# A hybrid encoder layer on one core: input weights loaded three units ahead, norms on VectorE, split tiles of the gated unit kept in DRAM, part of V made later, and w_down's squares spread out

## The chip, the cores and the metric

The kernel runs on one core of a Trainium2 chip. A core has a matrix engine (TensorE, PE in the profile; PEld is its weight load), VectorE (DVE), ScalarE (ACT), GpSimd (POOL), and SyncE (SP), which here only issues DMAs. Each engine works through a queue of its own in order; semaphores tie the queues together. Sixteen DMA engines move data between DRAM and the core's on-chip memory. The metric is the time of one execution on the device in microseconds.

## The reference

The layer computes, for a sequence of 2048 tokens of width 1024 and a memory of 256 tokens:

```python
y = rmsnorm(h, norm_mix_g) @ w_in            # 1024 -> 3*512 (q, k, v) + 2*512 (a, g)
q, k = partial_rotary(q), partial_rotary(k)  # 16 of 64 columns of each head
att = dilated_sliding_attention(q, k, v)     # patterns (128, 1), (512, 4), (2048, 16)
conv = silu(layernorm(conv31(a * sigmoid(g))))
h = h + concat(att, conv) @ w_out
h = h + softmax(xq @ xk.T / 16) @ xv @ w_xo  # xq of rmsnorm(h), xk and xv of rmsnorm(mem)
u = rmsnorm(h, norm_mlp_g) @ w_up            # 1024 -> 4096
h = h + square(relu(u)) @ w_down
out = rmsnorm(h, norm_final_g)
```

All inputs and outputs are float32. Attention has 8 heads of 64, its three patterns are merged with their log-denominators; cross attention has 4 heads of 256.

## The kernel before, in words

**Numbers as pairs.** A float32 product is made of three float16 products: each operand is scaled by a power of two and split into a hi and a lo part, and `mm3` (L392 to L394) issues hi·hi, hi·lo and lo·hi. So each weight tile of 128 output columns (a "raw" tile of 128 x 8 x 128, 0.5 MB) has to be loaded, scaled and split before TensorE can use it. For the input weights w_in the scale comes from the tile itself: `wscale` (L322) squares it and sums the squares on ScalarE (`wjunk`), a one-column matmul `p` (L198) sums over partitions, and a few small instructions of VectorE and GpSimd (`pow2`) make the scale. `wsplit16` (L345) then scales the tile in place on ScalarE (L349), casts it to the hi part (L351) and subtracts on GpSimd or VectorE (L352). For the later weights `wsplit2` (L379) does it in two instructions, with scales that come from sums of squares over whole matrices: `scan` reads w_up and w_out once for that (40 tiles, `sjunk`, L225) while the first stages run, and `scan_down` reads w_down (32 tiles, `sjunkd`, L247).

**Stages in time.** (1) Memory: the fold of w_xq, w_xk, w_xv and w_xo with the memory's norm into two matrices per head that are put into DRAM as ascr and bscr (results `pa`, `pb`, evicted into `eb`, squared for their scale at L670). (2) `xprep`: x is read in four blocks of 512 tokens; `rstd_nat` (L510) takes the squares of each row (`sumsq`, L505, `junk`), transposes of 128 x 128 (`xt`) turn it, VectorE multiplies it with gain and norm (`xv`, L540), ScalarE and GpSimd split it (`xh`, `xl`). `rb` and `rbs` are the norm broadcast over partitions. (3) The linear stage: `pipeline` (L700) runs units. A unit is one weight tile with what hangs on it: `glu` gives the units g and a of the four column groups c (their halves for token blocks 0, 1 here); `lin_qk` the units q and k, of which the pair named kr and qr holds the rotated columns of all heads, gathered from w_in in 64-byte pieces with eight DMAs each; `lin_v` (L775) the two halves of V, 256 columns each. Results go to DRAM (`uscr`, `kscr`, `qscr`, `qfar`, `vtok`). (4) The far stretch: attention of block 0 with its farthest pattern (`att(0)`; scores `s`, probabilities `sm`, transposes `pt`, its split `ph`, `pl`, output `opt`), in which the other halves of g and a (token blocks 2, 3), with their weights loaded, scaled and split again, serve as filler (`rest`). (5) Four times a `post` block of 512 tokens: w_out, cross attention (`x`, `xs`, `xp`), then w_up and w_down, with the attention and the convolution of the next block woven in. `scan_down` runs at the start of the first.

**What sets the order.** A step of a unit is what its generator does up to the next `yield`: load, square, scale, split, then matmuls. `pipeline` advances the next unit and the one after beside the current one, so that a load is two units ahead; the raw buffers are two. `weave(main, (side, rate))` advances a side generator by `rate` steps for each step of the main one. Within this, a scheduler of the framework puts the instructions of each engine in order by its own estimate of their times, except where `pinned` and `after` fix that a group is issued after the last marked instruction of an engine. All loads and nearly all stores go through SyncE's queue in that order; a store there waits at the head of the queue until its data is ready. Some stores of q and k are issued by ScalarE.

Of the kernel before, what the change touches and what calls it, by code (L numbers as in the profile page):

```python
# [10 lines left out]
F32 = mybir.dt.float32  # L11
# [10 lines left out]
P = 128  # L22
# [26 lines left out]
def hybrid_layer(ctx, tc, A, out):  # L49
# [68 lines left out]
    catl = [dr.tile([P, S], F16, name=f"catl{k}") for k in range(KC)]  # L118
    ascr = dr.tile([XH // 2, P, KC, 2 * NMEM], F32, name="ascr")
# [150 lines left out]
    def bounds():  # L270
# [9 lines left out]
        with ExitStack() as st:  # L280
# [9 lines left out]
            DVE.scalar_tensor_tensor(c[14], c[4], 4.0, c[14], op0=ALU.mult, op1=ALU.add)  # L290
# [32 lines left out]
    def wscale(raw, key):  # L323

        if key in tiles_scaled:
            yield
            return
        n = tiles_scaled[key] = 4 * len(tiles_scaled)
        q = lp.tile([P, 1024], BF16, tag="wjunk", name="wjunk")
        ACT.activation(q, raw.rearrange("p a b -> p (a b)"), AF.Square, accum_out=wsc[:, n + 3:n + 4])  # L330
# [14 lines left out]
    def wsplit16(raw, key, name, lo_eng=None, views=None):  # L345
        hi = wp.tile([P, 8, P], F16, tag="whi", name=f"whi_{name}", bufs=2)
        lo = wp.tile([P, 8, P], F16, tag="wlo", name=f"wlo_{name}", bufs=2)
        s = wcol(key, 0)
        ACT.activation(raw, raw, AF.Copy, scale=s)  # L349
        for of, to in views or ((lambda t: t,) * 2,):  # L350
            ACT.copy(to(hi), of(raw))  # L351
            (lo_eng or DVE).tensor_tensor(to(lo), of(raw), to(hi), op=ALU.subtract)  # L352
        return hi, lo
# [25 lines left out]
    def wsplit2(wp, raw, name, scale, bufs=2, shape=(P, 8, P)):  # L379
        hi = wp.tile(list(shape), F16, tag="whi", name=f"whi_{name}", bufs=bufs)  # L380
        lo = wp.tile(list(shape), F16, tag="wlo", name=f"wlo_{name}", bufs=bufs)
        ACT.activation(hi, raw, AF.Copy, scale=scale)  # L382
        DVE.scalar_tensor_tensor(lo, raw, scale, hi, op0=ALU.mult, op1=ALU.subtract)  # L383
        return hi, lo
# [94 lines left out]
    xna[2] = pool("x2", stack=mems, side="right")  # L479
    XH_ = {}  # L480
# [24 lines left out]
    def sumsq(sp, t, ss, j, n):  # L505

        for e in range(2):
            q = sp.tile([P, 512], BF16, tag="junk", name="junk", bufs=1)
            ACT.activation(q, t[e], AF.Square, accum_out=ss[:, n * e + j:n * e + j + 1])

    def rstd_nat(sp, nat, name):
        n = len(nat)
        ss = sp.tile([P, 8], F32, tag="ss", name=f"ss{name}", bufs=2)
        for j in range(n):
            sumsq(sp, nat[j], ss, j, n)
# [33 lines left out]
    def memory(sp):  # L549
# [24 lines left out]
        def wtiles(name, shape=(P, 8, P)):  # L574
            i = cnt[0] % 4
            cnt[0] += 1
            if i < 2:
                return [wp.tile(list(shape), dt, tag=t, name=f"m{t}_{name}", bufs=2)
# [121 lines left out]
    def pipeline(*units):  # L700

        for _ in range(4):
            next(units[0])
# [1143 lines left out]
```

## Time and profile before

| | us |
|---|---|
| median of 3 runs | 2853.81 (2852.42 to 2854.03) |
| the profiled execution | 2859.55 |
| its span | 2857.8 |
| TensorE busy | 2702.5 (95%) |
| VectorE busy | 2017.9 (71%) |
| ScalarE busy | 1379.2 (48%) |
| GpSimd busy | 489.6 (17%) |
| moved by DMA | 455.80 MB, mean 159 GB/s |

The times of the profile are those of one execution, counted from its first instruction. A "granted clock" below 1 means that TensorE ran below its full rate for part of the stretch. In a row of waits the engine that waits stands first, then what it waited for, then the total, the number and the longest. In a row of the timeline the bracket at the end is the idle time ahead of the instruction and what ended it.

### The profile page before, as it was taken

The numbers are of one execution on the slowest core, as the hardware profiler recorded it, in microseconds if no ns is written. First come the engines' busy times: TensorE is split into PE (matmuls) and PEld (weight loads), VectorE is DVE, ScalarE is ACT, GpSimd is POOL, SyncE is SP. The second block draws the span as 40 slices with busy tenths as digits, with TensorE's granted clock in tenths as the row PEclk, the third lists the DMA queues.
The fourth block names the chain that finished last, engine by engine and source line by source line (L and its number), as shares of the span: only waits on it lengthen the run. The fifth ranks groups of instructions, "written<-read, shape, count | busy, mean of one in ns | idle before, by whom it ended". The sixth has DMA issues, their size and how long they took to land.

```text
span 2857.8 us, 41763 instructions
## 1 busy us (share of the span) xinstructions
PE 2702.5 (95%) x15482; PEld 1486.6 (52%) x15482; DVE 2017.9 (71%) x3647; ACT 1379.2 (48%) x2295; POOL 489.6 (17%) x521
## 2 busy tenths in 40 slices
PE   8878799998887999999999999999999999999998
PEld 7744346666644555554554555455455544444443
DVE  6534664565567798756799886679979655579997
ACT  5776422265566444443454445345434444455443
POOL 1135442222210111130002202200201130000000
PEclk9989899999998999999999999999999999999999
DMA  9899985568896354454544454553445445323332
GB/s 273 245 266 282 252 206 150 137 171 215 218 274 213 103 142 132 137 147 119 169 128 127 132 147 125 158 165 110 136 135 142 126 147 158 105 82 103 118 118 67
DMA packets 629773, 455.80 MB, mean 159 GB/s; under 512 B 192733, under 2 KB 558225, under 8 KB 629056
## 3 DMA queue, kind: packets, MB, share of 16 engines
q1 hardware_dynamic: 588816, 429.19, 53.5%
q10 hardware_dynamic: 38528, 17.93, 2.5%
q0 software_dynamic: 2224, 6.01, 0.6%
q8 instruction: 122, 2.00, 0.3%
q14 instruction: 83, 0.68, 0.1%
HBM read 370.04 MB, written 82.98 MB: 159 GB/s over the span
## 4 chain that ended last, share of the span: by engine, by line
PE 48%; DVE 3%; issue 2%; DMA 2%; POOL 1%; ACT 0%; SPq 0%; POOLq 0%; DVEq 0%; ACTq 0%
PE dn L392 6%; PE dn L394 6%; PE dn L393 6%; PE up L392 6%; PE up L393 6%; PE up L394 6%; PE o L392 1%; PE o L394 1%; PE o L393 1%; PE xs L392 1%; PE xs L394 1%; PE xs L393 1%; PE s L1236 1%; PE pt L1014 1%; DVE cacc L409 1%
## 5 line engine op out<-in xcount | busy, mean ns | idle before, releaser
L392 PE MATMUL up<-mh,whi_u 128*128 128x512 f16 x1024 | 389.4, 381 | 7.5 <-ACT mh L1460 3.8
L409 DVE SCALAR_TENSOR_TENSOR cacc<-cu,cw,cacc 128x512 f32<-128x512 f32 x480 | 387.5, 807 | 5.6
L393 PE MATMUL up<-ml,whi_u 128*128 128x512 f16 x1024 | 389.1, 380 | 1.2 <-DVE ml L1461 1.2
L394 PE MATMUL up<-mh,wlo_u 128*128 128x512 f16 x1024 | 387.9, 380 | 0.0
L394 PE MATMUL dn<-hhh,wlo_d 128*128 128x512 f16 x768 | 291.3, 380 | 0.0
L393 PE MATMUL dn<-hhl,whi_d 128*128 128x512 f16 x768 | 290.8, 380 | 0.0
L392 PE MATMUL dn<-hhh,whi_d 128*128 128x512 f16 x768 | 283.8, 380 | 0.1
L382 ACT ACTIVATE whi_u<-raw_u,bd 128x1024 f16<-128x1024 f32 x128 | 146.8, 1147 | 257.3 <-PE dn L393 163.8
L382 ACT ACTIVATE whi_d<-raw_d,bd 128x1024 f16<-128x1024 f32 x100 | 114.9, 1149 | 263.3 <-PE up L393 229.3
L383 DVE SCALAR_TENSOR_TENSOR wlo_u<-raw_u,bd,whi_u 128x1024 f16<-128x1024 f32 x128 | 169.5, 1324 | 33.8 <-ACT whi_u L382 33.6
L1586 DVE SCALAR_TENSOR_TENSOR h<-dn,bd,h 128x512 f32<-128x512 f32 x192 | 140.4, 745 | 72.8 <-PE dn L394 72.7
L394 PEld LDWEIGHTS <-wlo_u 128*128 128x128 f16 x1024 | 100.4, 98 | 121.6 <-issue 2.7
L1007 DVE CUSTOM_DVE_ANT_0 sm<-s,mask 128x256 f32<-128x256 f32 (+1 forms) x384 | 127.1, 374 | 51.0 <-PE s L1236 31.6
L393 PEld LDWEIGHTS <-whi_u 128*128 128x128 f16 x1024 | 100.7, 98 | 119.0 <-issue 6.3
L392 PEld LDWEIGHTS <-whi_u 128*128 128x128 f16 x1024 | 100.8, 99 | 116.2 <-issue 2.7
L369 POOL TENSOR_TENSOR nr<-st_v,mhalf 128x4 f32<-128x4 f32 (+1 forms) x15 | 17.3, 1152 | 825.3 <-DVE st_v L365 825.3
L1570 DVE SCALAR_TENSOR_TENSOR rl<-up,ssumx 128x512 f32<-128x512 f32 x96 | 65.7, 689 | 124.7 <-PE up L394 124.6
L383 DVE SCALAR_TENSOR_TENSOR wlo_d<-raw_d,bd,whi_d 128x1024 f16<-128x1024 f32 x100 | 132.9, 1329 | 23.1 <-ACT whi_d L382 22.8
L1018 DVE TENSOR_TENSOR pl<-pt,ph 128x512 f16<-128x512 f32 x160 | 109.4, 685 | 55.4 <-ACT ph L1017 55.0
L1008 ACT ACTIVATE sm<-sm,o 128x256 f32<-128x256 f32 (+1 forms) x288 | 116.6, 453 | 52.2 <-DVE o L1007 51.6
L1017 ACT CAST ph<-pt 128x512 f16<-128x512 f32 x160 | 91.2, 573 | 82.4 <-PE pt L1014 82.4
L394 PEld LDWEIGHTS <-wlo_d 128*128 128x128 f16 x768 | 75.3, 98 | 89.4 <-issue 1.0
(541 smaller groups left out, 6776.6 us busy)
## 6 DMA issues: line engine op xcount, KB each, us to landing
raw_u<-in_w_up_dram SPq DMA_DIRECT2D x128, 512.0 KB
raw_d<-in_w_down_dram SPq DMA_DIRECT2D x100, 512.0 KB
scan<-in_w_up_dram SPq DMA_DIRECT2D x32, 512.0 KB
raw_o<-in_w_out_dram SPq DMA_DIRECT2D x32, 512.0 KB
scand<-in_w_down_dram SPq DMA_DIRECT2D x32, 512.0 KB
raw_a<-ascr SPq DMA_DIRECT2D x32, 512.0 KB
raw_b<-bscr SPq DMA_DIRECT2D x32, 512.0 KB
b<-in_w_down_dram SPq DMA_DIRECT2D x28, 512.0 KB
```

The costliest lines, as they stand in the source:

```text
L382: ACT.activation(hi, raw, AF.Copy, scale=scale)
L383: DVE.scalar_tensor_tensor(lo, raw, scale, hi, op0=ALU.mult, op1=ALU.subtract)
L392: PE.matmul(o, lh, rh, start=first, stop=False, skip_group_check=more)
L393: PE.matmul(o, lh, rl, start=False, stop=False, skip_group_check=more)
L394: last["pe"] = PE.matmul(o, ll, rh, start=False, stop=end, skip_group_check=more)
L409: DVE.scalar_tensor_tensor(acc, u[:, t:t + 512], cw[:, c, t:t + 1], acc, op0=ALU.mult, op1=ALU.add)
L1007: last["dve"] = DVE.tensor_tensor_reduce(dst, so, mask[:, 256 * m:256 * m + nk], 1.0, 3e38, ALU.add, ALU.min, mn)
L1008: last["act"] = ACT.activation(dst, dst, AF.Exp, bias=mn, scale=-1.0)
L1017: ACT.copy(ph, pt)
L1018: DVE.tensor_tensor(pl, pt, ph, op=ALU.subtract)
L1570: last["dve"] = DVE.scalar_tensor_tensor(r, pt, 0.0, rsb, op0=ALU.max, op1=ALU.mult)
L1586: last["dve"] = DVE.scalar_tensor_tensor(hs[m], pt, K_DN, hs[m], op0=ALU.mult, op1=ALU.add)
```

## The change

The change has eight parts.

1. Loads: three raw buffers in place of two; `pipeline` starts the load of unit i + 3 when unit i begins (units 0, 1 and 2 are advanced 4, 3 and 1 steps ahead of the first).
2. Squares and norms: `wscale` takes the largest square of each partition with one VectorE instruction in place of the sum on ScalarE; the same for the squares of `eb` (their bound's factor goes from 4 to 16 for it); the rows' sums of squares of token blocks 2 and 3 go to VectorE too.
3. Splits: q, k, g and a are split as the later weights are, by one scaled cast on ScalarE and one subtraction with scale on VectorE; only kr and qr keep the old form. Hi and lo part are the halves of one tile `ws` (two buffers). The memory stage's split tiles get a pool of their own.
4. The gated unit's eight split tiles of the first pass are stored into `gscr` in DRAM, and the second pass, in the far stretch, reads them (`wr_`) in place of loading, scaling and splitting.
5. V: of the second pair only token blocks 0 and 1 are made in the linear stage; its split weights are stored into `vscr`, read again (`wvr1`), and token blocks 2 and 3 are made as the first unit of the far stretch's filler.
6. Filler: the attention steps of the far stretch take 1.0 step of filler each in place of 0.75.
7. Rates of `scan` and of the first convolution steps in the linear stage.
8. `scan_down`: 1 step per step of the first 12 of the block, then 1.25 over the next 18, in place of 4 per step over 9 steps after those 12.

```diff
     def wscale(raw, key):
-        if key in tiles_scaled:
-            yield
-            return
         n = tiles_scaled[key] = 4 * len(tiles_scaled)
         q = lp.tile([P, 1024], BF16, tag="wjunk", name="wjunk")
-        ACT.activation(q, raw.rearrange("p a b -> p (a b)"), AF.Square, accum_out=wsc[:, n + 3:n + 4])
+        w = raw.rearrange("p a b -> p (a b)")
+        DVE.tensor_tensor_reduce(q, w, w, 1.0, 0.0, ALU.mult, ALU.max, wsc[:, n + 3:n + 4])
...
-    def wsplit16(raw, key, name, lo_eng=None, views=None):
-        hi = wp.tile([P, 8, P], F16, tag="whi", name=f"whi_{name}", bufs=2)
-        lo = wp.tile([P, 8, P], F16, tag="wlo", name=f"wlo_{name}", bufs=2)
-        s = wcol(key, 0)
-        ACT.activation(raw, raw, AF.Copy, scale=s)
-        for of, to in views or ((lambda t: t,) * 2,):
-            ACT.copy(to(hi), of(raw))
-            (lo_eng or DVE).tensor_tensor(to(lo), of(raw), to(hi), op=ALU.subtract)
-        return hi, lo
...
+    def wsplit2(wp, raw, name, scale, shape=(P, 8, P)):
+        t = wp.tile([P, 2, *shape[1:]], F16, tag="ws", name=f"ws_{name}", bufs=2)
+        ACT.activation(t[:, 0], raw, AF.Copy, scale=scale)
+        DVE.scalar_tensor_tensor(t[:, 1], raw, scale, t[:, 0], op0=ALU.mult, op1=ALU.subtract)
+        return t
...
-    def sumsq(sp, t, ss, j, n):
+    def sumsq(sp, t, ss, j, n, dve):
         for e in range(2):
             q = sp.tile([P, 512], BF16, tag="junk", name="junk", bufs=1)
-            ACT.activation(q, t[e], AF.Square, accum_out=ss[:, n * e + j:n * e + j + 1])
+            o = ss[:, n * e + j:n * e + j + 1]
+            if dve:
+                DVE.tensor_tensor_reduce(q, t[e], t[e], 1.0, 0.0, ALU.mult, ALU.add, o)
+            else:
+                ACT.activation(q, t[e], AF.Square, accum_out=o)
...
-                    ACT.activation(q_, ev, AF.Square, accum_out=acc2[:, i_:i_ + 1])
+                    DVE.tensor_tensor_reduce(q_, ev, ev, 1.0, 0.0, ALU.mult, ALU.max, acc2[:, i_:i_ + 1])
...
     def pipeline(*units):
+        def go(i, n=1):
+            for _ in range(n if i < len(units) else 0):
+                next(units[i])
+        for i, n in enumerate((4, 3, 1)):
+            go(i, n)
         for i, u in enumerate(units):
+            go(i + 1)
+            go(i + 3)
             for j, _ in enumerate(u):
                 if j == 0:
-                    next(nxt, None)
+                    go(i + 2)
                 yield
-            next(nxt, None)
+            go(i + 2)
...
         def unit(x, c0):
+            again = (x, c) in tiles_scaled
+            if not again:
+                raw = wp.tile([P, 8, P], F32, tag="raw", name=f"raw_{x}{c}{ns[0]}", bufs=3)
+                dma(raw, wcols(w_in, c0))
+            yield
+            if again:
+                w = wp.tile([P, 2, 8, P], F16, tag="raw", name=f"wr_{x}{c}{ns[0]}", bufs=3)
+                dma(w, gscr[2 * c + (x == "a")])
+                yield
+            else:
+                yield from wscale(raw, (x, c))
+            yield
+            if not again:
+                w = wsplit2(wp, raw, f"{x}{c}{ns[0]}", wcol((x, c), 0))
+                dma(gscr[2 * c + (x == "a")], w)
+            wh, wl = two(w)
...
-    def lin_v(g, ns):
+    def lin_v(g, ns, again=False, fine=False):
...
+        if again:
+            wv = lbv.tile([P, 2, 8, 256], F16, tag="wv", name=f"wvr{g}")
+            dma(wv, vscr)
...
+        if not again and ns[-1] < NG - 1:
+            dma(vscr, wv)
...
-        steps = pipeline(*units, *glu(2, early01), lin_v(0, alln), *glu(3, early01), lin_v(1, alln))
+        steps = pipeline(*units, *glu(2, early01), lin_v(0, alln), *glu(3, early01), lin_v(1, early01))
...
-        weave(islice(steps, 31), (vsc, 0.42), (conv0, 0.58), (scn, 0.4))
+        weave(islice(steps, 31), (vsc, 0.42), (conv0, 0.58), (scn, 0.75))
...
+        lbv = pool("far_v", stack=st)
-        rest = pinned(pipeline(*(u for c in range(4) for u in glu(c, (2, 3), True)), ahead(0), ahead(1)), "pe")
+        rest = pinned(pipeline(lin_v(1, (2, 3), True, True), *(u for c in range(4) for u in glu(c, (2, 3), True)), ahead(0), ahead(1)), "pe")
...
-        weave(islice(first, 50), (ln0, 0.33), (rest, 0.75))
+        weave(islice(first, 50), (ln0, 0.33), (rest, 1.0))
...
-            weave(islice(main_, 4), (first, 2))
-            weave(islice(main_, 8), (first, 0.5))
+            weave(islice(main_, 4), (first, 2), (dsc, 1))
+            weave(islice(main_, 8), (first, 0.5), (dsc, 1))
...
-            weave(islice(main, 9), (dsc, 4), *sides)
+            weave(islice(main, 18), (dsc, 1.25), *sides)
```

More of the change, by code (lines that the diff above doesn't have):

```diff
@@ L118, in hybrid_layer @@
     catl = [dr.tile([P, S], F16, name=f"catl{k}") for k in range(KC)]
+    gscr = [dr.tile([P, 2, 8, P], F16, name=f"gscr{i}") for i in range(8)]
+    vscr = dr.tile([P, 2, 8, 256], F16, name="vscr")
     ascr = dr.tile([XH // 2, P, KC, 2 * NMEM], F32, name="ascr")
@@ L846, in lin_qk @@
             yield
-            hi, lo = wsplit16(raw, key, nm, lo_eng=POOL)
+            hi, lo = two(wsplit2(wp, raw, nm, wcol(key, 0)))
         def rope(n):
@@ L944, in edges @@
     def edges():
-        zrow = wp.tile([64, 1, VR], F16, tag="raw", name="zrow", bufs=2)
+        zrow = wp.tile([64, 1, VR], F16, tag="raw", name="zrow", bufs=3)
         DVE.memset(zrow, 0.0)
```

72 lines of the change are left out of this document (32 added, 40 removed).

## The prediction

> **What bounds the kernel now.** I read the page first, then a table by stage, then the waits of the stages that lose time.
>
> ```profile
> span 2857.8 us, 41763 instructions
> PE 2702.5 (95%) x15482; PEld 1486.6 (52%) x15482; DVE 2017.9 (71%) x3647; ACT 1379.2 (48%) x2295; POOL 489.6 (17%) x521
> ```
>
> ```profile
> 104.00:133.00 29.00, 24.96 (x101) 19.03 (x101) 8.76 (x14) 27.84 (x60) 1.01 (x1) 0.94 0.71 200
> 133.00:235.00 102.00, 75.42 (x334) 39.84 (x333) 43.49 (x98) 79.57 (x147) 40.21 (x35) 0.80 1.02 276
> 235.00:330.00 95.00, 73.54 (x332) 33.07 (x331) 46.78 (x70) 52.40 (x78) 46.98 (x46) 0.89 1.03 264
> 445.00:555.00 110.00, 107.30 (x879) 85.94 (x878) 63.87 (x128) 27.82 (x50) 18.71 (x38) 1.00 0.54 147
> 555.00:779.00 224.00, 197.27 (x1753) 149.88 (x1752) 125.51 (x531) 131.44 (x310) 58.46 (x74) 0.94 0.73 190
> 779.00:975.00 196.00, 165.03 (x910) 87.03 (x906) 127.65 (x253) 112.84 (x206) 16.62 (x19) 0.89 0.71 208
> ```
>
> The columns are stretch, length, busy time of PE, PEld, DVE, ACT, POOL, granted clock, DMA share, GB/s. TensorE is the bound of the whole (95%), so only its idle and slow stretches can be won. Four of them bear on this change: the fold of memory (104 to 133), the linear stage (133 to 330), the far stretch (555 to 779) and the start of the first post block (779 to 975). Their idle time is 4.0 + 26.6 + 21.5 + 26.7 + 31.0 = 110 us, from length less PE busy. ScalarE is all but full in the first (27.84 of 29), and in the linear stage the DMA engines are full (share 1.02, 1.03).
>
> ```profile
> PE lin L392 <- ACT whi_q L351: 11.2, 1, 11.2
> PE xt L535 <- DVE xv L540: 10.2, 7, 3.0
> PE p L198 <- ACT rbs L530: 7.5, 2, 3.9
> PE p L198 <- DVE vs L766: 7.1, 1, 7.1
> PE lin L392 <- ACT whi_kr L351: 5.8, 1, 5.8
> ACT wjunk L330 <- DMA raw_qr<-in_w_in_dram: 9.8, 2, 5.6
> ACT sjunk L225 <- DMA kscr<-sth_k: 7.7, 1, 7.7
> ```
>
> Those are the waits of TensorE and ScalarE in 133 to 330 (total, times, longest). ScalarE's queue is what holds TensorE: it stands in front of weights that have not landed, or behind its own stores.
>
> **The change, part by part.**
>
> *Squares and norms to VectorE.*
>
> ```profile
> L330 ACT ACTIVATE wjunk<-raw_g x4: 1057/1058/1065, 116.2 to 453.8; 128x1024 bf16<-128x1024 f32 x4
> L509 ACT ACTIVATE junk<-xn 128x512 bf16<-128x512 f32 x24 | 14.9, 622 | 0.6 <-DMA xn<-in_x_dram 0.4
> L670 ACT ACTIVATE junk<-eb 128x512 bf16<-128x512 f32 x16 | 10.0, 626 | 0.2
> L670 ACT ACTIVATION_READ_ACCUMULATOR junk<-eb 128x1 f32 x16 | 3.0, 189 | 0.0
> L1007 DVE CUSTOM_DVE_ANT_0 sm<-s,mask 128x128 f32<-128x128 f32 x128 | 30.2, 286 | 17.5 <-PE s L1091 15.7 <-DMA oscr<-o 1.2
> L1007 DVE CUSTOM_DVE_ANT_0 sm<-s,mask 128x256 f32<-128x256 f32 x60 | 23.0, 421 | 7.5 <-PE s L1236 7.1
> PE pb L392 <- ACT eb L667: 4.0, 3, 2.5
> ```
>
> ScalarE loses 16 squares of eb, 13.0 us, 16 of the x norms (x2 and x3) at 0.622 + 0.189 = 13.0 us, and 16 of weight tiles at 1.058 + 0.19 = 20 us. The nearest VectorE row with a reduction is the masked maximum of the scores: 286 ns for 128 columns and 421 for 256, 1.05 ns a column; carried on, an estimate of 0.69 us for 512 and 1.23 for 1024. So VectorE takes about 22 us for the 32 short ones and 20 for the weights. In 104 to 133 it is busy 8.76 of 29 us and takes its 16 without delay; ScalarE goes from 28 to about 15 of 29, and the 4.0 us that pb waits for eb are the most that can go. I take −3 (0 to −4).
>
> *The splits of q, k, g, a.*
>
> ```profile
> L349 ACT ACTIVATE raw_g<-raw_g,wsc x8: 1133/1148/1150, 139.3 to 610.2; 128x1024 f32<-128x1024 f32 x8
> L352 POOL TENSOR_TENSOR wlo_g<-raw_g,whi_g x8: 2124/2128/2138, 143.6 to 677.0; 128x1024 f16<-128x1024 f32 x8
> L383 DVE SCALAR_TENSOR_TENSOR wlo_u<-raw_u,bd,whi_u 128x1024 f16<-128x1024 f32 x128 | 169.5, 1324 | 33.8 <-ACT whi_u L382 33.6
> ```
>
> Scale in place, cast and GpSimd's 2.13 us become one scaled cast (1.15, as for w_up) and 1.32 us on VectorE: about 1.9 us less from scale to lo part for each of 14 first splits, and 14 × 2.13 us leave GpSimd. kr and qr keep their strided form, now on one tile. Hi and lo as halves of one tile change only the reuse: a buffer comes free with the last reader of either half, within one block of matmuls.
>
> *Loads three units ahead, 133 to 235.*
>
> ```profile
> 190.85 8.08 SPq L58 DMA_DIRECT2D raw_kr<-in_w_in_dram  x8
> 199.03 6.27 SPq L58 DMA_DIRECT2D raw_qr<-in_w_in_dram  x8
> 225.55 0.61 PE L392 MATMUL lin<-xh,whi_kr 128*128 128x512 f16 x1 [5.80 <-ACT whi_kr L351]
> DMA packets 107371, 53.84 MB, mean 269 GB/s; under 512 B 58103, under 2 KB 97052, under 8 KB 107359
> ```
>
> raw_kr's eight issues move ahead of glu 1's tail, raw_qr's ahead of the last x loads; the scans, the xscr stores and the xn loads that stood before them on SyncE now stand behind. The lead is real, but the bytes are the same in a window where the 16 engines are full (the last row is for 130 to 330), and four stores of split tiles of g and a (0.5 MB each, 2 MB at 269 GB/s = 7.8 us of the engines) come on top, each at the head of SyncE's queue until its lo part is done. Against that ScalarE loses its 9.8 us of waits and about 25 us of work. On VectorE, however, the squares of raw_qr and raw_k0 stand ahead of the last squares of x3, and so ahead of its reciprocal norm. I put the gain and the cost at even: 0, between −25 (nearly all of the 26.6 idle us) and +16 (first rival).
>
> *235 to 330.*
>
> ```profile
> 303.65 6.72 ACTq L58 DMA_DIRECT2D kscr<-sth_k  x3
> ```
>
> The split of q0 still stands on ScalarE behind these three stores, which end at 310.4. Before, scale, cast and two squares of the scan came between there and the 11.2 us wait's end; after, one square less and a scaled cast in place of scale and cast: 1.25 + 1.04 us less, of which I count 1.7 because the lo part then waits for VectorE. With a little more from the other units, −4 (−18 if the 11.2 and 7.1 waits go, +5 if VectorE's rope chain falls behind the squares).
>
> *Half of V's second pair moved.*
>
> ```profile
> L392 PE MATMUL up<-mh,whi_u 128*128 128x512 f16 x1024 | 389.4, 381 | 7.5 <-ACT mh L1460 3.8
> ...
> 549.74 0.27 PE L392 MATMUL v<-wvh,xh 128*128 128x256 f16 x1
> ...
> 550.39 0.27 PE L392 MATMUL v<-wvh,xh 128*128 128x256 f16 x1
> ```
>
> Eight token tiles of 24 matmuls, 192, leave a dense stage (107.30 of 110) and enter the start of the far stretch: the work itself costs nothing. From the first to the last of the seven matmuls between the two rows are 0.65 us, 0.108 each, so 20.8 us move. But its weights are stored (1 MB) and read again into a tile that lies where the old one lay, so the read starts after TensorE's last V matmul, behind the store of that tile's V on SyncE, and TensorE's next instruction needs it: nothing else is in its queue. Eviction and issue of about 2 us and 1.05 MB at 190 to 276 GB/s, 3.8 to 5.5 us, give 6 to 8 us idle; then the clock is low, as at 225.55, where a 512-wide matmul takes 0.61 us where up, of the same width, has a mean of 0.38, and some 2 us more are lost. +9 (0 if the read were somehow early; +14 if the 10.3 us that a 0.5 MB tile took at 662.97, below, is the rule).
>
> *Split tiles of g and a re-read in the far stretch.*
>
> ```profile
> 662.97 1.15 ACT L349 ACTIVATE raw_a<-raw_a,wsc 128x1024 f32<-128x1024 f32 x1 [10.27 <-DMA raw_a<-in_w_in_dram]
> 664.46 0.77 PE L1014 MATMUL pt<-ident,sm 128*128 128x128 f32 x2 [8.43 <-ACT sm L1008]
> PE pt L1014 <- ACT sm L1008: 13.6, 3, 8.4
> ```
>
> ScalarE stood 10.27 us in front of raw_a with the softmax of the attention behind it, and TensorE idled 8.43. After, no ScalarE or GpSimd instruction of this stretch touches a g or a tile; TensorE itself waits for it, one buffer and one unit further ahead. −11: 8.43 and some 2.5 us of low clock behind it (0 if TensorE then waits as long; −14 with all of sm's 13.6). ScalarE's other gain, 8 × (1.15 + 1.04) us, hides behind TensorE. Next late is the remaining 5.2 us of sm's waits, for the softmax itself, which stays.
>
> *Filler.* The attention steps of the far stretch get 1.0 step of linear work each in place of 0.75, and the work lasts: some 21 us more of it, what V displaces from the 38 steps ahead. The rest of the 26.7 idle us there is in waits of under 5 us: −3 (0 to −6).
>
> *Squares of w_down.*
>
> ```profile
> ACT sjunkd L247 <- DMA scand<-in_w_down_dram: 24.5, 18, 4.2
> L247 ACT ACTIVATE sjunkd<-scand 128x1024 bf16<-128x1024 f32 x32 | 33.7, 1053 | 24.6 <-DMA scand<-in_w_down_dram 24.5
> PE opt L1022 <- ACT ph L1017: 9.8, 4, 3.4
> ```
>
> 32 squares, 33.7 us, were put four to a step, and ScalarE's queue stood 24.5 us in front of them with ph behind. Spread over 30 steps from the block's start, about one to a step, a wait for one can hold ph less. Half of the 9.8 us of opt and its low clock: −6 (−15 if xs and x waits go too; +5 if the loads, now begun earlier, meet those of catl and raw_b). Scans of w_up at a higher rate, conv rates and zrow's third buffer change nothing on TensorE's path: 330 to 555 is dense. Their bound is ±5.
>
> **Sum.** −3 + 0 − 4 + 9 − 11 − 3 − 6 = −18. The profiled run took 2859.55 us (span 2857.8 and 1.75 around it), 5.74 above the median of 2853.81. 2841.5 by the profile, 2836 as a median.
>
> **Rivals.**
>
> *VectorE's queue stands in front of unlanded weights.* The squares take their wait along. raw_kr and raw_qr took 8.08 + 6.27 us to issue and raw_k0 1.9 us at 269 GB/s; if raw_k0 lands after x2's last xv, x3's norm and TensorE's xt wait up to 16.3 us, and the squares of q0 and k1 hold the rope multiplies likewise, by the 10.27 of raw_a: 26 us, 2862. For it: DMA share 1.02. Against: the loads stand some 25 instructions earlier on SyncE, and VectorE is busy 43.49 of 102. It decides once raw_k0 lands later than about 205.
>
> *VectorE and GpSimd in each other's way.*
>
> ```profile
> L409 DVE SCALAR_TENSOR_TENSOR cacc<-cu,cw,cacc x20: 729/752/2498, 284.3 to 329.7; 128x512 f32<-128x512 f32 x20
> ```
>
> The same multiply-add took 752 ns as a median and 2498 once, 1.75 us more, next to GpSimd's work. About 25 squares move into 133 to 330, where GpSimd is busy 87 of 197 us: 25 × 0.44 × half of 1.75 = 10 us, on the path if all of it delays xv or xl: 2846. Against: 14 GpSimd splits of 2.13 us go, and they are the longest of its operations. The Trainium skill ("SBUF — State Buffer", Who interferes with whom) states that a VectorE instruction with two SBUF inputs and a GpSimd one that reads SBUF exclude each other, the later waiting for the whole of the earlier; the row of 2498 agrees, and by the rule a square is such an instruction, so that the sum would be 2841 to 2846 in place of 2836.
>
> *The linear stage opens up.* With ScalarE free, half of its 48 idle us and some 4 us of low clock go: 28 us more, 2808. Against: DMA share.
>
> *The re-read tiles land late*, and TensorE waits directly: −11 and −3 become 0, 2850. For it: 6 MB more traffic (4 of g and a stored, 1 of V stored and 1 re-read). Against: the DMA share of that stage is 0.73, and a re-read takes the place of a read of the same size.
>
> **How the numbers follow.** Forecast 0.42 (own range 2822 to 2848); VectorE's queue 0.20; GpSimd 0.10; linear stage opens 0.13; late tiles 0.10; others 0.05. What can be told from no change is 0.2%, 2848.1 to 2859.5. Faster: 0.42 + 0.10 + 0.13 and 0.03 of the others, 0.68. Same: late tiles, 0.10. Slower: 0.20 and 0.02, 0.22. The range reaches from the open linear stage with its best far stretch, 2804, to just past the first rival, 2864.
>
> **What would show it.** Right: pb no longer waits for eb; no wait of ScalarE for raw_a and no gap near 8 us in the far stretch; one wait of TensorE's v matmuls for wvr1 of 6 to 8 us at its start; the kr matmuls begin within 222 to 231 us; sjunkd's waits shorter. Wrong: xt waiting on VectorE norms after squares with a DMA releaser; TensorE waiting for wr tiles; or PE idle in 133 to 330 well under 40 us.

## The result, and the profile after

The changed kernel takes 2831.6 us (median of 4 runs, 2827.49 to 2834.45) where the kernel before takes 2853.11 (4 runs). The ratio is 0.9923, with a 95% interval of 0.9906 to 0.9941: some 22 us less, 17 to 27. The profiled execution took 2834.45 us with a span of 2832.7; against the profiled execution before the span is 25.1 us shorter. Both profiled executions are slower than the medians, the changed kernel's by 2.9 us and the one before by 6.4, so the differences between the two profiles add up to some 4 us more than the gain itself.

The first part of the page of the changed kernel:

```profile
span 2832.7 us, 41746 instructions
PE 2692.5 (95%) x15482; PEld 1486.3 (52%) x15482; DVE 2063.9 (73%) x3757; ACT 1311.4 (46%) x2169; POOL 451.7 (16%) x499
```

TensorE runs the same 15,482 matmuls. It is busy 10.0 us less (fewer of them at a low clock) and idle 15.1 us less (span less busy: 155.3 before, 140.2 after). ScalarE has 68 us less to do, GpSimd 38 less, VectorE 46 more.

The two traces are laid beside each other at moments that both have, the first or last matmul into a named tile. Between two of them TensorE has the same work, except that 20.8 us of V move from the fifth row to the sixth.

| from, to | before, us | after, us | difference |
|---|---|---|---|
| start, last pxv | 104.2 | 106.5 | +2.3 |
| to last pb (fold of memory) | 29.3 | 24.5 | −4.8 |
| to first kr matmul | 92.1 | 99.6 | +7.5 |
| to first q0 matmul, to last q matmul | 89.1, 107.2 | 88.5, 107.9 | −0.6, +0.7 |
| to last V matmul of this stage | 131.7 | 110.0 | −21.8, with the 20.8 of V −1.0 |
| to first o matmul (far stretch) | 225.5 | 244.3 | +18.8, with the 20.8 of V −2.0 |
| to first up matmul (start of the first post block) | 197.6 | 184.8 | −12.8 |
| to first ot matmul | 372.8 | 361.6 | −11.2 |
| to the end of the span | 1508.3 | 1505.0 | −3.2 |

They add up to −25.1 (each is rounded by itself). Ten of the runs below have everything up to the last pxv as the changed kernel has it, and there it lasts 103.0 to 105.3 us: differences of 2 us in a row belong to the execution and not to the change.

The table by stage of the changed kernel (stretch, length, busy time of PE, PEld, DVE, ACT, POOL, granted clock, DMA share, GB/s):

```profile
104.00:131.00 27.00, 25.22 (x119) 20.20 (x118) 18.41 (x39) 20.51 (x40) 1.31 (x1) 1.00 0.82 232
131.00:231.00 100.00, 68.03 (x298) 36.75 (x297) 65.42 (x149) 48.44 (x76) 30.74 (x28) 0.76 1.03 281
231.00:319.00 88.00, 68.85 (x306) 31.38 (x304) 49.14 (x68) 48.33 (x72) 44.18 (x40) 0.89 1.03 271
537.00:781.00 244.00, 219.30 (x1945) 171.18 (x1946) 140.51 (x551) 126.22 (x309) 44.99 (x74) 0.94 0.75 199
781.00:966.00 185.00, 157.90 (x920) 84.40 (x918) 132.93 (x262) 115.08 (x209) 19.55 (x20) 0.93 0.73 224
966.00:1100.00 134.00, 132.13 (x773) 69.17 (x772) 119.35 (x196) 56.89 (x89) 31.54 (x33) 1.00 0.46 132
1100.00:1328.00 228.00, 228.00 (x1225) 113.78 (x1224) 157.21 (x242) 99.95 (x142) 41.80 (x41) 1.00 0.49 139
```

The first post block's start (781 to 966) is idle 27.1 us where it was 31.0 in 779 to 975, and its clock rose from 0.89 to 0.93: of the 12.8 us of this row 3.9 are idle time, and the rest is busy time, shorter at the higher clock. From 1100 to 1328 TensorE is never idle. In the linear stage the DMA share is 1.03 as before, ScalarE is no longer full, and TensorE is idle 32.0 us from 131 to 231, more than the 26.6 of before.

TensorE's waits in the fold of memory, then in 131 to 231, then in the far stretch:

```profile
PE pb L392 <- ACT eb L672: 1.4, 2, 0.7
```

```profile
PE rb L375 <- DVE rsx L370: 8.5, 2, 4.4
PE xt L540 <- DMA xn<-in_x_dram: 5.3, 2, 4.0
PE xt L540 <- DVE p2s L206: 4.6, 3, 2.7
PE lin L392 <- ACT ws_kr L349: 2.1, 1, 2.1
```

```profile
PE v L392 <- DMA wvr<-vscr: 10.9, 1, 10.9
PE pt L1036 <- ACT sm L1030: 7.3, 2, 4.1
PE s L1112 <- DMA qh<-qfar: 2.5, 2, 2.3
```

The first shows the fold without its wait (4.0 us before). The second shows the new wait of the linear stage: the norm of x, now on VectorE. The third has the predicted wait for V's weights first, and no wait that comes from a raw g or a tile.

### The profile page after: what moved, and what is told of

Read it like the earlier page. It is cut to its first block, busy times and chain, and to the rows that moved or that the text cites. A ratio compares the mean times of both kernels' runs of the same rounds, so it can differ in the third digit from the quotient of the medians.

```text
span 2832.7 us, 41746 instructions
## 1 busy us (share of the span) xinstructions
PE 2692.5 (95%) x15482; PEld 1486.3 (52%) x15482; DVE 2063.9 (73%) x3757; ACT 1311.4 (46%) x2169; POOL 451.7 (16%) x499
## 4 chain that ended last, share of the span: by engine, by line
PE 76%; DMA 9%; DVE 6%; ACT 3%; issue 2%; SPq 2%; POOL 1%; ACTq 1%; POOLq 0%; DVEq 0%
PE up L392 7%; PE up L393 7%; PE up L394 7%; PE dn L392 7%; PE dn L394 7%; PE dn L393 7%; PE pt L1036 2%; PE s L1258 2%; PE lin L392 2%; PE lin L393 2%; PE xs L392 2%; PE xs L393 2%; PE x L392 2%; PE xs L394 2%; PE x L393 2%
## 5 line engine op out<-in xcount | busy, mean ns | idle before, releaser
L392 PE MATMUL up<-mh,ws_u 128*128 128x512 f16 x1024 | 389.6, 381 | 2.6 <-DVE rl L1593 2.6
L393 PE MATMUL up<-ml,ws_u 128*128 128x512 f16 x1024 | 389.4, 380 | 0.0
L394 PE MATMUL up<-mh,ws_u 128*128 128x512 f16 x1024 | 388.3, 380 | 0.0
L393 PE MATMUL dn<-hhl,ws_d 128*128 128x512 f16 x768 | 290.2, 379 | 0.3 <-DVE hhl L1596 0.3
L394 PE MATMUL dn<-hhh,ws_d 128*128 128x512 f16 x768 | 290.1, 379 | 0.0
L392 PE MATMUL dn<-hhh,ws_d 128*128 128x512 f16 x768 | 283.2, 379 | 0.8 <-DVE h L1609 0.8
L379 ACT ACTIVATE ws_u<-raw_u,bd 128x1024 f16<-128x1024 f32 x128 | 146.8, 1147 | 244.8 <-PE dn L394 199.7
L379 ACT ACTIVATE ws_d<-raw_d,bd 128x1024 f16<-128x1024 f32 x100 | 114.9, 1149 | 280.7 <-PE up L394 248.7
L380 DVE SCALAR_TENSOR_TENSOR ws_u<-raw_u,bd,ws_u 128x1024 f16<-128x1024 f32 x128 | 168.4, 1315 | 18.2 <-ACT ws_u L379 17.7
L394 PEld LDWEIGHTS <-ws_u 128*128 128x128 f16 x1024 | 100.5, 98 | 120.4 <-issue 1.6
L393 PEld LDWEIGHTS <-ws_u 128*128 128x128 f16 x1024 | 100.9, 99 | 116.7 <-issue 4.0
L392 PEld LDWEIGHTS <-ws_u 128*128 128x128 f16 x1024 | 100.6, 98 | 115.6 <-issue 1.6
L380 DVE SCALAR_TENSOR_TENSOR ws_d<-raw_d,bd,ws_d 128x1024 f16<-128x1024 f32 x100 | 134.5, 1345 | 29.1 <-ACT ws_d L379 28.4
L394 PEld LDWEIGHTS <-ws_d 128*128 128x128 f16 x768 | 75.1, 98 | 89.1 <-issue 0.6
```

Source lines behind the costliest of these rows:

```text
L379: ACT.activation(t[:, 0], raw, AF.Copy, scale=scale)
L380: DVE.scalar_tensor_tensor(t[:, 1], raw, scale, t[:, 0], op0=ALU.mult, op1=ALU.subtract)
L392: PE.matmul(o, lh, rh, start=first, stop=False, skip_group_check=more)
L393: PE.matmul(o, lh, rl, start=False, stop=False, skip_group_check=more)
L394: last["pe"] = PE.matmul(o, ll, rh, start=False, stop=end, skip_group_check=more)
```

## The experiments

Each run is compared with runs of the kernel before on the same chip, whose medians there were 2855.7 to 2859.4; so the ratios are what is compared, with the changed kernel's 0.9923. One thousandth is 2.9 us.

| run | ratio | 95% interval |
|---|---|---|
| the changed kernel | 0.9923 | 0.9906 to 0.9941 |
| e, old rates of w_down's squares | 0.9988 | 0.9976 to 1.0 |
| p, the new rates alone on the kernel before | 0.9961 | 0.9947 to 0.9975 |
| b, V second in the filler | 0.9894 | 0.9875 to 0.9913 |
| c, V whole in the linear stage | 0.9938 | 0.9924 to 0.9953 |
| d, no DRAM copies of g and a | 0.9877 | 0.9861 to 0.9893 |
| s, copies stored, not read | 0.9905 | 0.9889 to 0.9922 |
| j, as d, loads two units ahead | 0.9937 | 0.9923 to 0.995 |
| f, norms of x2 and x3 on ScalarE | 0.9909 | 0.9893 to 0.9926 |
| a, scan loads behind q and k weights | 0.9948 | 0.9932 to 0.9964 |
| l, scan loads behind kr and qr, V second | 0.9929 | 0.9916 to 0.9942 |
| k, scan loads behind all weights, V second | 0.9935 | 0.992 to 0.9949 |
| m, as d with V second | 0.9838 | 0.9817 to 0.9858 |

**The spread of w_down's squares, taken out and put in alone.**

```diff
-            weave(islice(main_, 4), (first, 2), (dsc, 1))
-            weave(islice(main_, 8), (first, 0.5), (dsc, 1))
+            weave(islice(main_, 4), (first, 2))
+            weave(islice(main_, 8), (first, 0.5))
...
-            weave(islice(main, 18), (dsc, 1.25), *sides)
+            weave(islice(main, 9), (dsc, 4), *sides)
```

> The changed kernel with the old rates of w_down's squares (4 per step over 9 steps after the first 12). By my sum the spreading gives 6 us: 2838. Rival 1 (all of what the first post block gained up to the first w_up matmul, 12.8 us, and the 11.2 us gained from there to 1350, hang on it): about 2855, with a wait of catT for GpSimd's cat of some 5 us back in the middle of the first w_up and w_down stretch. Rival 2 (the gain there comes from the other parts): within 3 us of 2832.

Measured: 0.9988, some 19 us above the changed kernel's ratio, as the first rival had it. In p the same lines are put the other way into the kernel before:

> The kernel before with one edit, the spread of w_down's squares (1 step per step over the first 12, then 1.25 over 18). Taking it out of the changed kernel cost about 20 us (2855.0 against 0.9923 of the kernel before on that chip, 2835). If that part carries nearly the whole gain, it gives about as much alone: 17 to 22 us, a ratio of 0.992 to 0.994, without the wait of catT for GpSimd's cat between 1195 and 1350. If it only repairs what the other parts upset: 0 to 8 us, a ratio above 0.997.

Measured: 0.9961, 11 us (7 to 15), between the two expectations. (The profiled execution of p is 4.4 us below its median, so its stages, laid beside those of the profile before, show more than that: 18 us.) From first o to first up p takes 185.6 us and e 195.3, where the kernel before took 197.6 and the changed one 184.8. The stage from first up to first ot lasts 372.8 us before, 376.6 in e, 366.8 in p and 361.6 in the changed kernel. The chain between attention's merge and its transposes is where it differs most; TensorE's waits between first up and first ot, before, in e and in the changed kernel:

```profile
PE catT L1181 <- POOL cat L1173: 4.9, 1, 4.9
```

```profile
PE catT L1203 <- POOL cat L1195: 6.6, 1, 6.6
PE up L392 <- ACT mh L1483: 2.3, 1, 2.3
PE s L1258 <- DMA qh<-qscr: 1.9, 1, 1.9
```

```profile
PE dn L392 <- DVE h L1609: 0.8, 1, 0.8
PE opt L1044 <- ACT ph L1039: 0.7, 1, 0.7
```

The wait for GpSimd's merge is in this stage in the two kernels with the old rates and in none of the twelve others. So it hangs on the rates, though the rates belong to work that is over long before: `weave` advances the sides (the next block's attention and convolution) with the steps of the block, the squares stand between them, and the merge's place in GpSimd's queue changes. That the wait comes and goes with the rates is shown; by which step of the queue is not.

At the start of the block itself the waits of ScalarE for the squares' loads hardly changed; ScalarE's waits in 781 to 966 of the changed kernel, and TensorE's there and in the same stage of e:

```profile
ACT sjunkd L249 <- DMA scand<-in_w_down_dram: 21.6, 19, 3.2
```

```profile
PE o L393 <- DMA catl<-catl: 7.8, 2, 5.6
PE xs L392 <- ACT xp L1523: 5.4, 1, 5.4
PE opt L1044 <- ACT ph L1039: 4.3, 2, 4.0
```

```profile
PE opt L1044 <- ACT ph L1039: 7.9, 3, 3.7
```

24.5 us became 21.6, but ph behind it is waited for 4.3 us in place of 9.8 (7.9 in e). The longest single wait for a square's load was 4.2 us and is 3.2.

**Half of V's second pair.** In c, V is whole again in the linear stage and the filler's rate is 0.75; the DRAM copies stay.

```diff
-        ... *glu(3, early01), lin_v(1, early01))
+        ... *glu(3, early01), lin_v(1, alln))
...
-        rest = pinned(pipeline(lin_v(1, (2, 3), True, True), *(...
+        rest = pinned(pipeline(*(...
...
-        weave(islice(first, 50), (ln0, 0.33), (rest, 1.0))
+        weave(islice(first, 50), (ln0, 0.33), (rest, 0.75))
```

> The changed kernel without the V part: the second pair of V is made whole in the linear stage, no store and re-read of its weights, filler at 0.75 as before. By my sum the V part costs 9 for its wait and the longer filler gives 3, so without it 6 us less, 2826 (2820 to 2831). Rival (the filler is worth more than the wait costs, because the attention's own waits in the far stretch are covered): 2835 to 2850.

Measured: 0.9938; 4 us slower than the changed kernel, with overlapping intervals, but clear of the 6 us gain of my sum. The profile tells more than the total. From the last V matmul to the first o matmul it takes 224.8 us in c, as in the kernel before (225.5), and 210.7 in the changed kernel. TensorE's waits there in c:

```profile
PE pt L1036 <- ACT sm L1030: 11.1, 2, 6.2
PE s L1112 <- DMA qh<-qfar: 5.7, 1, 5.7
PE s L1112 <- DVE o L1029: 5.3, 2, 4.9
```

So with the copies but without V in the filler the far stretch gains nothing. ScalarE no longer stands in front of a raw tile of g or a, but other waits have taken the place of that one: TensorE is idle 26.8 us in this stretch, as before (26.7), and its waits for the softmax are 11.1 us (13.6 before, 7.3 in the changed kernel). The changed kernel is idle 24.8 us there, 13.9 without the wait for V's weights.

In b the order within the filler changes, so that V's weights are read while g0 is computed:

```diff
+        units2 = [u for c in range(4) for u in glu(c, (2, 3), True)]
+        units2.insert(1, lin_v(1, (2, 3), True, True))
-        rest = pinned(pipeline(lin_v(1, (2, 3), True, True), *(...), ahead(0), ahead(1)), "pe")
-        for _ in range(38):
+        rest = pinned(pipeline(*units2, ahead(0), ahead(1)), "pe")
+        for _ in range(50):
...
-        weave(islice(first, 50), (ln0, 0.33), (rest, 1.0))
+        weave(islice(first, 50), (ln0, 0.33), (rest, 0.93))
```

> The changed kernel with one edit: in the far stretch's filler the unit g0 comes first and the second half of V after it, with 50 steps ahead of the attention in place of 38 and filler at 0.93 in place of 1.0. My prediction's step (TensorE waits for the re-read of V's weights because nothing else is in its queue): the 10.9 us wait for wvr1 and its low clock go, 9 to 12 us less, about 2821. Rival (the wait only moves: g0's re-read tile is not there either, or the attention's loads then come late): within 4 us of the changed kernel.

Measured: 0.9894, 8 us less, near the expectation (the intervals overlap a little); in its profile the wait for wvr1 is 0.8 us in place of 10.9, and the first o matmul starts 8.5 us earlier (772.7).

**The DRAM copies of g and a.** In d the far stretch loads w_in again and splits it with the stored scale, and nothing is stored.

```diff
-            if not again:
-                raw = wp.tile(...)
-                dma(raw, wcols(w_in, c0))
+            raw = wp.tile(...)
+            dma(raw, wcols(w_in, c0))
...
-                w = wp.tile([P, 2, 8, P], F16, tag="raw", name=f"wr_{x}{c}{ns[0]}", bufs=3)
-                dma(w, gscr[2 * c + (x == "a")])
...
-            if not again:
-                w = wsplit2(wp, raw, f"{x}{c}{ns[0]}", wcol((x, c), 0))
-                dma(gscr[2 * c + (x == "a")], w)
+            w = wsplit2(wp, raw, f"{x}{c}{ns[0]}", wcol((x, c), 0))
```

> The changed kernel without the DRAM copies of the gated unit's split tiles: the far stretch loads w_in again and splits it with the stored scale (one scaled cast on ScalarE, one subtraction on VectorE), nothing is stored in the first pass. By my sum the copies give 11 us in the far stretch: 2842 to 2847, with ScalarE waiting some 10 us for a raw tile there. Rival (the three raw buffers and the longer lead alone take that wait away, and the four stores in the linear stage's full DMA window cost as much as they give): 2825 to 2834.

Measured: 0.9877; the copies cost 13 us in place of giving 11. TensorE's waits from the last V matmul of the linear stage to the first o matmul, in d:

```profile
PE v L392 <- DMA wvr<-vscr: 11.4, 1, 11.4
PE s L1107 <- DMA qh<-qfar: 5.0, 1, 5.0
PE pt L1031 <- ACT sm L1025: 3.2, 1, 3.2
```

TensorE's 8 us wait for the softmax does not come back though the raw tiles are loaded and split there again. In s the tiles are stored but not read:

```diff
+            w = wsplit2(wp, raw, f"{x}{c}{ns[0]}", wcol((x, c), 0))
+            if not again:
+                dma(gscr[2 * c + (x == "a")], w)
```

> The changed kernel with the eight split tiles of g and a still stored in the first pass, but not read: the far stretch loads w_in again and splits it. Without stores and re-reads the time was 0.9877 of the kernel before, with both 0.9923. If the stores cost it (2 MB into the full DMA window of the linear stage and a place at the head of SyncE's queue): 0.991 to 0.993, 2830 to 2835. If the re-reads cost it (TensorE's far stretch waits for the split tiles, where ScalarE and VectorE have time to split them anyway): 0.987 to 0.989, 2820 to 2825.

Measured: 0.9905, under the upper expectation's 0.991 and above the lower one's 0.989, between the two. The stores would account for some 8 us of the 13 and the re-reads for 5, but its interval overlaps both neighbours. The profiles, one execution each, agree on where it happens: the last V matmul of the linear stage ends at 536.7 in s, as in the changed kernel (536.9), and at 529.0 in d; from there to the first o matmul it takes 237.6 in s and 240.9 in d against 244.3. So the stores delay the linear stage and the re-reads the far stretch; how the 13 us divide stays open.

**The lead of the loads.** j is d with the old `pipeline` and two raw buffers everywhere.

> The run without DRAM copies, with the old lead: two raw buffers and loads two units ahead. If it is the third buffer and the longer lead that took ScalarE's 10 us wait for a raw tile out of the far stretch, as the run without copies suggests, the wait and the 8 us gap of TensorE come back there, and the linear stage loses little or gains (its DMA window is full either way): 2829 to 2842, 0.990 to 0.995. If the lead does nothing and the change of the filler moved the waits: within 4 us of 2823.

Measured: 0.9937, 17 us above d. But the 10 us wait for a raw tile in the far stretch did not come back, so the expectation was right in size and wrong in place. The last V matmul of the far stretch comes 10.6 us later than in d, of which 1.7 are there at the last q matmul, 8.0 arise up to the last V matmul of the linear stage and 0.9 after it; 13.5 us are left at the end of the span, of which 7.3 arise after the first ot matmul.

With c this tells what took the idle time out of the far stretch. Without its wait for V's weights TensorE is idle there 13.9 us in the changed kernel, 12.5 in d and 11.4 in j, which has neither the copies nor the lead, but 26.8 in c, which has both and the old filler. So it was the other filler. The attention's steps now have g and a matmuls beside them at 1.0 step each, because V took the first 32 of the steps ahead; whether the rate does it or V's place in front, no run tells apart.

j shows one thing more. The post blocks load their weights into the same raw buffers, and the third buffer counts there too. From first ot to the end of the span the three kernels with two raw buffers take 1508.3 us (before), 1510.4 (p) and 1511.3 (j), the eleven with three 1503.3 to 1505.6. ScalarE's waits for raw_u tiles behind 1330 us are 37.4, 40.8 and 37.3 us with two buffers, and 4.3 in the changed kernel and in d. From first up to first ot, with the new rates of w_down's squares, it is 366.8 (p) and 365.6 (j) against 361.6 to 362.0 in the ten with three.

**The norms.** f puts the squares of x2 and x3 back on ScalarE:

```diff
-            sumsq(sp, nat[j], ss, j, n, name in ("x2", "x3"))
+            sumsq(sp, nat[j], ss, j, n, False)
```

> The changed kernel with the squares of x2 and x3 back on ScalarE; the weights' squares stay on VectorE. By my first rival VectorE's queue stands before unlanded weights with x3's norm behind: between 131 and 231 the broadcast rb waits 4.5 and 4.1 us for the norm. With the norms on ScalarE, whose queue now holds little in that stage, kr begins 4 to 8 us earlier than 230.5 and the time falls by as much, to 2824 to 2828. If those waits come from x tiles that land late (an xn transfer is waited for 9.1 and 3.2 us by VectorE), the squares wait on ScalarE just as long: within 3 us of 2832.

Measured: 0.9909, 4 us less, not clear of the changed kernel. kr begins at 227.5, 3 us earlier; but in b, c and e, which have everything up to there as the changed kernel has it, it begins at 228.3 to 230.3. Counted from the last pxv matmul kr comes after 123.1 us in f, after 124.0 to 127.0 in the changed kernel, b, c and e, and after 121.3 before, so f takes back 1 to 4 us of what was lost up to there. The rest of the wait moved: in f TensorE waits 5.3 us for rsx and 9.7 for rbs, in the changed kernel 8.5 and 4.1. VectorE's queue in the changed kernel shows what is late (start, duration, idle before it and its releaser):

```profile
202.08 1.23 DVE L330 CUSTOM_DVE_ANT_0 wjunk<-raw_qr 128x1024 bf16<-128x1024 f32 x1 [4.43 <-DMA raw_k<-in_w_in_dram]
...
205.13 1.23 DVE L330 CUSTOM_DVE_ANT_0 wjunk<-raw_k 128x1024 bf16<-128x1024 f32 x1 [1.82 <-DMA raw_k<-in_w_in_dram]
...
213.45 0.69 DVE L512 CUSTOM_DVE_ANT_0 junk<-xn 128x512 bf16<-128x512 f32 x1 [3.21 <-DMA xn<-in_x_dram]
```

The queue does stand in front of raw_qr and raw_k0, as my first rival said, for 6.2 us (the first bracket names raw_k, whose loads were issued right behind the last piece of raw_qr, at 198.8). But x3's last tile lands at 213.4, after them: SyncE issued it at 206.3 to 209.5, behind raw_qr, raw_k0 and three scan loads, where the kernel before issued its last x load at 189.9, ahead of raw_kr. That transfer is late, whichever engine squares it.

**Fewer transfers in the linear stage.** a keeps the 40 scan loads on SyncE behind the loads of q and k weights (`dma` returns its instruction, the loads of lin_qk are marked, and the scan's steps are pinned to them):

```diff
-    scn = chain(scan(scp), bounds())
+    scn = chain(pinned(scan(scp), "sp"), bounds())
...
-                dma(raw[:, :, p:p + m], ...
+                last["sp"] = dma(raw[:, :, p:p + m], ...
```

> The changed kernel with the 40 scan loads of w_up and w_out (20 MB) kept behind the loads of the q and k weights on SyncE, so that they no longer stand in front of x loads and weights between 130 and 230 us. Theory A (the linear stage is bound by the DMA engines: share 1.03, and TensorE's waits there for x, norms and weights come from late transfers): 20 MB at 273 GB/s is 73 us of transfer taken out of a window of 200 us; TensorE's idle time from 131 to 319, 51 us, falls by a third to two thirds, and the time falls by 17 to 35 us, to about 2797 to 2815. Theory B (the waits are the serial chain of square, norm and broadcast on VectorE, not transfers): within 5 us of the changed kernel. A cost of up to 10 us is possible under both if the scales of w_up come later than they are needed.

Measured: 0.9948, 7 us more than the changed kernel, though theory A held for the stage it spoke of: kr begins at 210.4 (230.5) and q0 at 295.0 (319.0). Its stages, and TensorE's waits after 295:

```profile
129.00:210.00 81.00, 61.59 (x301) 33.41 (x300) 65.80 (x152) 28.33 (x38) 34.04 (x29) 0.89 0.74 205
210.00:295.00 85.00, 71.21 (x298) 30.57 (x298) 48.51 (x63) 40.81 (x59) 42.30 (x39) 0.88 0.91 229
295.00:415.00 120.00, 112.70 (x500) 50.79 (x500) 65.55 (x109) 36.88 (x53) 36.27 (x43) 0.93 0.96 235
415.00:450.00 35.00, 23.77 (x104) 10.60 (x104) 20.04 (x42) 12.01 (x19) 8.48 (x16) 0.88 0.98 254
```

```profile
PE v L392 <- DMA wvr<-vscr: 11.5, 1, 11.5
PE lin L392 <- ACT ws_g L379: 5.1, 1, 5.1
PE v L392 <- ACT wv L811: 4.4, 1, 4.4
PE lin L392 <- ACT ws_q L379: 4.2, 1, 4.2
```

With a DMA share of 0.74 from 129 to 210 the stage is 20 us shorter. The bytes come back later: from the first q0 matmul to the last V matmul of the linear stage the DMA share is 0.91 (295 to 543) where the changed kernel has 0.78 (319 to 537), and TensorE is idle 24.5 us there in place of 4.0. By the last V matmul of the far stretch the 24 us have turned into 8 lost. l holds the scans only behind kr and qr, k behind all input weights, both with V second:

> The changed kernel with V second in the filler (as in the run before, 9 us less) and the 40 scan loads held on SyncE only behind the loads of kr and qr. In the run with all scan loads behind every q and k weight the first q matmul began 24 us earlier (295.0 against 319.0) and the gain was lost again in the V stage, where weights then waited behind scan loads. If the early part of the linear stage is what the scans hold up, and the V stage is left alone: 10 to 20 us under the run with V second, 2805 to 2816. If the bytes only move the wait within the same stage: within 5 us of that run, 2821 to 2831.

> As the run before, but the scan loads held behind the loads of all input weights, those of g, a and V too. If in the run with scans behind q and k weights alone the V stage lost its 20 us because g, a and V weights stood behind scan loads, they now stand ahead of them: 2800 to 2815. If the V stage loses because the DMA engines or ScalarE have the scans' work then, whatever the order of issue: 2830 to 2840.

Measured: 0.9929 and 0.9935, both worse than b (0.9894). In l q0 begins at 307.0, in k at 294.0, and both have lost it by the end of V (575.0 and 578.8 against 571.9 in b). Holding the scans back moves the wait; where they would fit better was not found.

**Both edits that helped.** m takes d and b together:

> The two edits that helped together: no DRAM copies of the split tiles of g and a (0.9877 of the kernel before) and V second in the filler (0.9894, where the changed kernel had 0.9923). If they take different time away, stores in the full DMA window and the 11 us wait for wvr1, they add: 0.9848, 2812 where the kernel before takes 2856. If V second needs g0's tile early, which a reload and a split now delay: no better than without copies, 2820 to 2826.

Measured: 0.9838 (0.9817 to 0.9858), 2807.99 us where the kernel before took 2859.4 on that chip: they add, and the result is faster than both kernels. V's first matmul of the far stretch no longer waits for its weights, only 0.77 us for `sig` on ScalarE, which reads a bank that the matmuls fill:

```profile
539.70 0.28 PE L392 MATMUL v<-wvr,xh 128*128 128x256 f16 x1 [0.77 <-ACT sig L747]
```

Parts 3 and 7 and the squares of the weights and of `eb` in part 2 have no run of their own.

## Why the prediction was right, and where it was not

The forecast of 2836 came within 5 us of 2831.6, inside its own range of 2822 to 2848, but by terms that erred both ways. Of its signs, pb's wait, raw_a's wait, the 8 us gap and TensorE's waits for wr tiles were as stated, kr began at 230.5, just inside 222 to 231, and the wait for wvr1 was 10.9 us and not 6 to 8.

- *Fold of memory, −3.* Right: −4.8 by the table above, and pb's wait went from 4.0 to 1.4 us. It is a little more than the 4.0 that I had as the most, and the clock of the stretch, 0.94 before, was 1.00.
- *133 to 235, 0.* +7.5. The mechanism was the one named as its risk and first rival, VectorE's queue in front of raw_qr and raw_k0 (4.43 and 1.82 us), together with x tiles that land late; by f, which takes back 1 to 4 us, the queue is one part of it, and how large a part stays open. The rival's 26 us were not reached.
- *235 to 330, −4.* −0.6. A kscr issue of 8.6 us on ScalarE in place of 6.7 would account for the 1.7 that I had counted; no run shows that it does.
- *V's re-read, +9.* Right in size: 10.9 us of idle time, and b took 8 us of it away. SyncE issued the load only at 542.2, 5.3 us after the end of the last matmul, and it landed 5.6 us later; I had 2 us and 3.8 to 5.5.
- *Copies, −11, and filler, −3.* The sum was nearly right (−12.9 in the far stretch without V and its wait), the step was wrong. The copies gave nothing there (c) and cost 13 us in all (d); the filler, which I had at 3, took the idle time away. The failing sentence was that after the change "no ScalarE or GpSimd instruction of this stretch touches a g or a tile", so the gap goes: it also goes when they do (d, j), and where they do not touch them but the filler is the old one, other waits fill its place (c).
- *w_down's squares, −6.* Right in sign, too small. By the table −12.8 up to the first up matmul; in all some 19 us by e, and 11 by p, where the rest of the change is missing.
- *Rest, 0 ±5.* −11.2 after that, and −3.2 from first ot on. The step that failed was to call the stage from first up to first ot free of the change. Its wait for GpSimd's merge and the low clock behind it were 7.5 us of loss there (4.9 idle, 2.6 from 5.1 us at a granted clock of 0.50) and hung on the rates of the part before. And the third raw buffer, which I counted in the linear stage alone, gives 4 to 5 us there (p and j against the others) and 3 to 7 behind it.

So one term was mis-sized, the squares with −6 for −11 to −19, one was put at nothing, the third buffer in the post blocks, and the copies had the wrong sign, −11 for +13. These errors nearly cancel: that the total came so close is in that respect luck.

*VectorE beside GpSimd*, my second rival, shows in the squares:

```profile
L330 DVE CUSTOM_DVE_ANT_0 wjunk<-raw_g x4: 1218/1226/1356, 106.8 to 451.0; 128x1024 bf16<-128x1024 f32 x4
L330 DVE CUSTOM_DVE_ANT_0 wjunk<-raw_q x3: 1219/1785/1912, 251.1 to 360.8; 128x1024 bf16<-128x1024 f32 x3
L512 DVE CUSTOM_DVE_ANT_0 junk<-xn x16: 673/688/1644, 140.7 to 215.3; 128x512 bf16<-128x512 f32 x16
```

The three figures are the least, the median and the longest in ns. The undisturbed durations are the estimates of 1.23 and 0.69 us, and single ones are up to 0.96 us longer. Seven of the 32 squares are longer, by 4.8 us in all, so the rival's 10 us were not reached even if every one of them had held TensorE up. Each of the seven began while a GpSimd instruction ran: the square of 1.64 us ran from 145.46 to 147.10, beside GpSimd's subtraction xl from 145.07 to 146.55, and so ended 0.55 us behind it. Squares that began before an xl (at 140.71, 149.01, 152.64 and 193.19) took 0.67 to 0.69. Two that began beside a GpSimd power of one to four columns were not longer either (169.86 and 341.96).

The Trainium skill ("SBUF — State Buffer", Who interferes with whom) has the later of a VectorE instruction with two SBUF inputs and a GpSimd one that reads SBUF wait for the whole of the earlier. The trace agrees for the longer instructions: 146.55 and 0.69 make 147.24, 0.14 us from the measured end.

The longest multiply-add of the convolution was 2498 ns before, beside one of GpSimd's splits; in the changed kernel, where q, k, g and a are split on VectorE, it is 1666.

## What to carry to other kernels

In a stretch where the DMA engines were full (share 1.03), saving ScalarE's work bought nothing here, and taking 20 MB out made it shorter but moved the wait to where the bytes went. A wait that goes away after a change of several parts is to be tried part by part before it is credited: here the idle time that the DRAM copies were to close was closed by the filler, and the copies themselves cost 13 us. A buffer added for one stage is to be counted in every stage that uses it. And a rate at which side work is woven in can decide a wait hundreds of microseconds later on an engine that the side work does not use.

## What the runs showed that was not expected

A read of 1.05 MB that TensorE waits for cost 10.6 to 12.8 us in the seven kernels that have V first in the filler, about half of it (5.3 of 10.9 us) before its issue on SyncE. One unit of 16 steps ahead of it took the wait to 0.2 to 1.5 us. Weights split again on ScalarE and VectorE in the far stretch cost TensorE no more than reading them ready-made from DRAM: the stretch takes 237.6 us (s) and 240.9 (d) with the splits, 244.3 with the reads, in one execution each.
